# One value group for all tokens in the first stage of a one-core decoder layer, the other group per half of the tokens

## The chip, the cores and the metric

The program runs on one core of one Trainium2 chip. The metric is the device time of one execution in microseconds (us): the kernel before takes 1529.22 us, the median of three runs (1527.17 to 1531.24). Of five engines, PE (TensorE) multiplies matrices into PSUM banks, DVE (VectorE) and POOL (GpSimd) do elementwise work, ACT (ScalarE) evaluates functions and copies, and SP (SyncE) issues nearly all DMAs. Each engine takes its instructions in a fixed order; so does SP's queue.

## What is computed

One layer over 1024 tokens of width 2048, conditioned by a vector c, all in float32:

```python
mod = silu(c) @ w_ada + b_ada
shift, scale, gate = split(mod, 3)
h = rms_norm(x, norm_g) * (1 + scale) + shift
u_a, v_a, z_a, q, k, v, z_b = split(h @ w_in)
y_a = u_a * (W_s LN(v_a) + b_s)
y_b = sliding_window_attention(rope(q), rope(k), v, sinks)
y = concat(y_a * silu(z_a), y_b * silu(z_b))
x = x + gate * (y @ w_out)
out = rms_norm(x, final_norm_g) * (1 + scale_f) + shift_f
```

LN is a layer norm over the 1024 columns of v_a (the "value columns" here); W_s mixes positions inside chunks of 128 tokens.

## The kernel before

**Arithmetic.** A float32 product is made of three faster ones: each operand is split into a rounded high part (ACT, a copy) and a low part (the difference, DVE or POOL), and `mm3` (lines 205 to 208) issues high x high, high x low and low x high into one bank. A projection of one 512-column group for one half (512 tokens) takes 16 steps of 128 input features (kt), each step 4 banks x 3 = 12 matmuls of 512 columns. `split_w` (lines 138 to 150) makes the parts of a weight step in three rotating buffers `wh`/`wl`; `chunk` (line 127) loads the weights of two steps by one 512 KB DMA.

**Stages.** The input tiles Hh, Hl (high and low) of only one half fit, so the halves run one after the other. At the start the modulation is not yet known: `scale` and `shift` are sums over 16 x 1 MB of w_ada that DVE makes step by step (`mod_col`, line 155, two multiply-and-sum instructions on line 165 per step, the data in ring buffers of 512 KB).

- The first stage (lines 655 to 675) projects half 0 for both value groups va0 and va1 as soon as each `scale` column is there: per kt the scale sums, the x tile, its split (lines 664 and 665), and two weight steps. The low weight parts of va0 go to POOL (from kt 2), those of va1 to DVE. It uses x * g * scale without the norm and the shift. Both are put in later: `norm_v` (line 438) multiplies by the row norm rx and adds the row shift @ W (the "correction"), on line 447, for half 0 only. Eight DMAs of rows of x also run here, for the norm (`x_stat`, line 170).
- Then `spread` (line 187) turns the norms into a tile, and the second stage (lines 690 to 695) projects kv and q0 with the full h, while `shift` is summed.
- `half(h)` (line 747) does q1, for half 1 also va0 and va1, then zb0, zb1, u0, u1, za0, za1 and the output projection.

**Order of the work.** Attention is a generator of 32 units (plus 3 steps to drain) that runs between the projection steps: `tick` (line 242) adds a credit per step, from kt 6 of q1 on, and lets one unit go when it reaches 1; the credit is 0.74 in half 0 and 0.58 in half 1 (line 774). A unit is scores (335, 336), soft-max (339 to 348), transposes (355), a split (359, 360) and values (367 to 376). A second queue of background work, `bg` (line 257), takes one step per two kt, by the lists `bgn`: first `corr_bg` (line 711: 16 loads of va weights, 32 sums on line 723, four loads of quarters of the shift row, then the sums become a row through bank `pv_bank`, which the attention's values also use), then `gate_bg` (32 sums, then a row through the bank mm[3]), then the x rows of half 1. A scheduler then sets each engine's order from the program order and priorities.

In half 0 all low weight parts from q1 to u0 are made on POOL (`lo_pool`), otherwise on DVE.

Of the kernel before, what the change touches and what calls it, by code (L numbers as in the profile page):

```python
# [10 lines left out]
F32 = mybir.dt.float32  # L11
# [4 lines left out]
P = 128  # L16
# [15 lines left out]
def R(t):  # L32
    return t.bitcast(F32R)
# [3 lines left out]
def hybrid_layer(ctx: ExitStack, tc: tile.TileContext, A, out):  # L37
# [7 lines left out]
    def st(shape, name):  # L45
        return sb.tile(shape, F32, tag=name, name=name)
# [391 lines left out]
    def norm_v(h):  # L438
        assert not waiting
        if h == 0:  # L440
            for i in range(2):
                load_row(4, i, zz[i])
        for t in range(4):
            va = [Y[t][:, i, :] for i in range(2)]
            if h == 0:
                for i in range(2):
                    dve.scalar_tensor_tensor(va[i], va[i], rx[0][:, t:t + 1], zz[i], op0=ALU.mult, op1=ALU.add)
                yield
# [81 lines left out]
    x_d = dram.tile([4, P, D], F32, name="x_d")  # L530
    r0 = st([P, 4], "rs0")
# [117 lines left out]
    acc, rb, sq = F[8], F[9], F[10:12]  # L649
    rings.extend(Y[1:4])  # L650
    raws.append(Y[0])

    stat0 = (None for t in range(4) for _ in x_stat(0, t))

    def g1_kt(kt):
# [9 lines left out]
        dve.scalar_tensor_tensor(R(Hl[kt]), X[kt], a, Hh[kt], op0=ALU.mult, op1=ALU.subtract)  # L665
        if kt >= 7:
            next(stat0, None)
        if kt == KT - 1:
            for _ in stat0:
# [3 lines left out]
    vb = project(["va0", "va1"], ["mm", "att"], per_kt=g1_kt, pool_lo=("va0",),  # L673
                 steps=[(kt, g) for kt in range(KT - 2) for g in ("va0", "va1")]
                 + [(kt, g) for g in ("va0", "va1") for kt in (KT - 2, KT - 1)])
    raws, rings = deque(w_raw), deque(ring)

    def g1_evac(i, t):
        grab(Y[t][:, i, :], vb[("va0", "va1")[i]][t])

    g1_evac(0, 0)
    with tc.high_priority():
        b = banks8["mm"][0]
        spread(rx[0], b, rb, sq[0])
    for i in range(2):
        for t in range(4):
            if i + t:
                g1_evac(i, t)
# [13 lines left out]
    def gate_bg():  # L702
        for kt in range(KT):
            yield from mod_col("gate", kt, gate_c[:, kt:kt + 1])
        to_row(0, gate_c, banks8["mm"][3])
# [5 lines left out]
    def corr_bg():  # L711
        to_row(3, shift_c, sc_bank[0])
        for pc in range(4):
            load_row(3, pc, misc)
            for c2 in range(4):
# [31 lines left out]
    def half(h, kq):  # L747
# [24 lines left out]
        def start(kt):  # L772
            if kt == 6:
                credit[0], credit[1] = 0.0, (0.74 if h == 0 else 0.58)
# [3 lines left out]
        if h:  # L778
            for i, g in enumerate(("va0", "va1")):
                ps = project([g], ["mm"], bgn=(0, 1))[g]  # L780
                for t in range(4):
                    grab(Y[t][:, i, :], ps[t])
# [130 lines left out]
```

## Time and profile before

| what | value |
|---|---|
| median of three runs | 1529.22 us |
| the profiled execution | 1529.09 us, span 1527.3 us |
| PE busy | 1457.6 us (95%), 7049 matmuls |
| DVE, ACT, POOL busy | 985.6, 630.9, 227.7 us |
| DMA | 284.85 MB, mean 187 GB/s |
| chain that ended last | PE 48%, issue 30%, DVE 10%, DMA 6% |

Matmuls are pipelined, so a busy PE in the table is not a PE at full rate: what counts is the time between the starts of two matmuls, and the idle stretches. "Granted clock" is the share of full TensorE speed; it has two levels, 1.0 (2.4 GHz) and 0.5 (1.2 GHz).

### The profile page before, as it was taken

What the parts mean: (1) busy time and instruction counts of PE and PEld (TensorE: products, weight loads), DVE (VectorE), ACT (ScalarE), POOL (GpSimd) and SP (SyncE); (2) the same over time, 40 slices, a digit from 0 to 9 for tenths busy, and PEclk for the clock granted to TensorE, in tenths of its full rate; (3) what the DMA queues carried; (4) which work ended last, traced back from release to release, by engine and by line L of the source; (5) the groups of instructions that cost most, each with busy time, mean ns of one, the idle gap of its engine ahead of it and who ended that gap; (6) DMA issues with size and microseconds to landing.
All of it is one profiled execution on the core that took longest, in us unless ns stands there. A gap on an engine that the chain in (4) does not pass through costs nothing.

```text
span 1527.3 us, 20341 instructions
## 1 busy us (share of the span) xinstructions
PE 1457.6 (95%) x7049; PEld 1209.2 (79%) x7049; DVE 985.6 (65%) x1953; ACT 630.9 (41%) x1397; POOL 227.7 (15%) x168
## 2 busy tenths in 40 slices
PE   7989999898899999999999999999999999999997
PEld 5768778676788887778889788788878888888897
DVE  6779864989854555533566578888755554456456
ACT  3443245566552233243343246566632222332341
POOL 1212154335341010000001010000011000010002
PEclk9999999999999999999999999999999999999999
DMA  9987855555334657665467664444355665565422
GB/s 364 354 286 240 266 185 154 169 179 183 86 120 147 198 181 237 212 206 171 158 191 232 193 208 143 124 138 124 120 186 181 204 203 190 173 226 194 136 86 111
DMA packets 89258, 284.85 MB, mean 187 GB/s; under 512 B 12145, under 2 KB 12737, under 8 KB 89154
## 3 DMA queue, kind: packets, MB, share of 16 engines
q1 hardware_dynamic: 89010, 283.02, 57.2%
q8 instruction: 55, 0.90, 0.2%
q10 hardware_dynamic: 144, 0.52, 0.1%
q14 instruction: 49, 0.40, 0.1%
HBM read 257.24 MB, written 13.67 MB: 177 GB/s over the span
## 4 chain that ended last, share of the span: by engine, by line
PE 48%; issue 30%; DVE 10%; DMA 6%; POOL 3%; ACT 2%; SPq 0%; DVEq 0%; POOLq 0%; ACTq 0%
PE mm L206 13%; PE mm L208 13%; PE mm L207 13%; DMA ring<-ada 2%; PE att L208 2%; PE att L207 2%; PE att L206 2%; DVE ring L165 1%; DVE ring L723 1%; PE att L355 1%; POOL wl L149 1%; DMA wr<-win 1%; DVE wl L149 1%; DVE t L339 1%; PE att L466 1%
## 5 line engine op out<-in xcount | busy, mean ns | idle before, releaser
L208 PE MATMUL mm<-r,wl 128*128 128x512 f32 x1024 | 402.6, 393 | 6.9 <-DVE wl L149 3.5
L206 PE MATMUL mm<-r,wh 128*128 128x512 f32 x1024 | 404.5, 395 | 1.1 <-ACT wh L148 0.4
L207 PE MATMUL mm<-r,wh 128*128 128x512 f32 x1024 | 402.8, 393 | 0.0
L148 ACT ACTIVATE wh<-wr 128x512 fp32r<-128x512 f32 x318 | 197.5, 627 | 332.2 <-PE mm L207 189.4
L149 DVE TENSOR_TENSOR wl<-wr,wh 128x512 fp32r<-128x512 f32 x226 | 164.6, 732 | 138.1 <-ACT wh L148 133.3
L208 PEld LDWEIGHTS mm<-r,wl 128*128 128x128 f32 x1024 | 194.2, 190 | 51.6 <-DVE wl L149 5.9
L206 PEld LDWEIGHTS mm<-r,wh 128*128 128x128 f32 x1024 | 194.2, 190 | 41.4 <-ACT y L285 1.3
L207 PEld LDWEIGHTS mm<-r,wh 128*128 128x128 f32 x1024 | 194.4, 190 | 37.5
L206 PE MATMUL mm<-wh,r 128*128 128x512 f32 (+1 forms) x448 | 170.5, 383 | 14.8 <-ACT r L664 12.0
L207 PE MATMUL mm<-wl,r 128*128 128x512 f32 (+1 forms) x448 | 171.2, 382 | 2.8 <-POOL wl L149 2.5
L148 ACT ACTIVATE wh<-ring 128x512 fp32r<-128x512 f32 x138 | 86.7, 629 | 207.4 <-PE mm L207 129.0
L149 POOL TENSOR_TENSOR wl<-wr,wh 128x512 fp32r<-128x512 f32 x92 | 129.5, 1411 | 283.1 <-ACT wh L148 237.7
L208 PE MATMUL mm<-wh,r 128*128 128x512 f32 (+1 forms) x448 | 168.4, 380 | 0.0
L207 PE MATMUL att<-wl,r 128*128 128x512 f32 (+1 forms) x448 | 161.3, 360 | 1.9 <-DVE wl L149 1.9
L208 PE MATMUL att<-wh,r 128*128 128x512 f32 (+1 forms) x448 | 160.8, 359 | 0.0
L206 PE MATMUL att<-wh,r 128*128 128x512 f32 (+1 forms) x448 | 160.7, 359 | 0.0
L149 DVE TENSOR_TENSOR wl<-ring,wh 128x512 fp32r<-128x512 f32 x138 | 97.7, 711 | 94.8 <-ACT wh L148 86.9
L206 PEld LDWEIGHTS mm<-wh,r 128*128 128x128 f32 x448 | 85.7, 192 | 35.1 <-ACT r L664 15.6
L480 POOL TENSOR_TENSOR y<-y,t 128x512 f32<-128x512 f32 x32 | 47.7, 1514 | 396.3 <-ACT t L489 351.1
L207 PEld LDWEIGHTS mm<-wl,r 128*128 128x128 f32 x448 | 85.9, 192 | 19.8 <-POOL wl L149 4.5
L208 PEld LDWEIGHTS mm<-wh,r 128*128 128x128 f32 x448 | 85.9, 192 | 16.0 <-DVE r L665 0.6
L207 PEld LDWEIGHTS att<-wl,r 128*128 128x128 f32 x448 | 84.4, 188 | 17.5 <-DVE wl L149 3.9
(207 smaller groups left out, 1984.2 us busy)
## 6 DMA issues: line engine op xcount, KB each, us to landing
wr<-win SPq DMA_DIRECT2D x124, 512.0 KB, 4.3
ring<-ada SPq DMA_DIRECT2D x90, 512.0 KB, 5.1
wr<-ada SPq DMA_DIRECT2D x55, 512.0 KB, 4.3
ring<-win SPq DMA_DIRECT2D x46, 512.0 KB, 3.8
wr<-wout SPq DMA_DIRECT2D x38, 512.0 KB, 3.7
ring<-wout SPq DMA_DIRECT2D x26, 512.0 KB, 3.7
y<-xn SPq DMA_DIRECT2D x20, 512.0 KB, 5.1
ring<-wvaT SPq DMA_DIRECT2D x16, 512.0 KB, 5.4
```

The costliest lines, as they stand in the source:

```text
L148: act.activation(R(w_hi[i]), r[:, kk, :], AF.Copy)
L149: (pool if on_pool else dve).tensor_tensor(R(w_lo[i]), r[:, kk, :], w_hi[i], op=ALU.subtract)
L165: dve.tensor_tensor_reduce(w, w, cb[:, c0:c0 + n], scale=1.0, scalar=prev, op0=ALU.mult, op1=ALU.add, accum_out=o)
L206: pe.matmul(o, lhsT=lh, rhs=rh, start=first, stop=False)
L207: pe.matmul(o, lhsT=lh, rhs=rl, start=False, stop=False)
L208: pe.matmul(o, lhsT=ll, rhs=rh, start=False, stop=last)
L339: dve.tensor_tensor_reduce(ps[i], os[i], mk, scale=-0.125, scalar=nsnk[:, h0 + i:h0 + i + 1], op0=ALU.add, op1=ALU.min, accum_out=nm[:, i: ...
L355: pe.transpose(pt_bank[:, c:c + P], p[:, 256 * i + P * j:256 * i + P * j + P], ident)
L466: pe.matmul(b[:, t * P:t * P + P], lhsT=Y[t][:, g // 4, (g % 4) * P:(g % 4) * P + P], rhs=wsp[:, g * P:g * P + P], start=True, stop=True)
L480: pool.tensor_tensor(y, y, zz[c], op=ALU.mult)
L723: dve.tensor_tensor_reduce(ti, ti, misc, scale=1.0, scalar=prev, op0=ALU.mult, op1=ALU.add, accum_out=acc_)
```

## The change

The first stage now projects va0 alone, but for both halves: x of both halves is loaded, scaled and split at each kt (`other` holds the parts of half 1), and one weight step serves both. Half 1's result is written to DRAM (`v_d`) and read back in half 1. The group va1 is projected in each half between q1 and zb0, with the full h, so it needs no correction. va0 is corrected in both halves, so the correction covers 512 columns (8 loads, 16 sums) and not 1024. The credit is 0.58 in both halves. The gate row goes through the bank `pv_bank` and, since the background list is shorter by 8 and half 0 longer by 8 calls, it falls into za0. All low parts of the first stage's weights from kt 2 on are POOL's.

```diff
--- before.py
+++ after.py
@@ -437,15 +437,11 @@
 
     def norm_v(h):
         assert not waiting
-        if h == 0:
-            for i in range(2):
-                load_row(4, i, zz[i])
+        load_row(4, 0, zz[0])
         for t in range(4):
             va = [Y[t][:, i, :] for i in range(2)]
-            if h == 0:
-                for i in range(2):
-                    dve.scalar_tensor_tensor(va[i], va[i], rx[0][:, t:t + 1], zz[i], op0=ALU.mult, op1=ALU.add)
-                yield
+            dve.scalar_tensor_tensor(va[0], va[0], rx[h][:, t:t + 1], zz[0], op0=ALU.mult, op1=ALU.add)
+            yield
             stt, mv, rs = sm(12, "bst"), sm(2, "mv"), sm(1, "rs")
             for i in range(2):
                 dve.bn_stats(stt[:, 6 * i:6 * i + 6], va[i])
@@ -528,6 +524,7 @@
         mm3(ps, R(Hh[f])[:, tk], R(Hl[f])[:, tk], Wh, Wl, first, last)
 
     x_d = dram.tile([4, P, D], F32, name="x_d")
+    v_d = dram.tile([4, P, 512], F32, name="v_d")
     r0 = st([P, 4], "rs0")
 
     def rows_bg(Am, Bm):
@@ -646,10 +643,11 @@
     dve.tensor_scalar(cols[:, C_B + 48:C_B + 64], cols[:, C_B + 48:C_B + 64], 1.0, None, op0=ALU.add)
 
     X = [F[i // 2] if i % 2 == 0 else Y[4 + i // 4][:, (i // 2) % 2, :] for i in range(KT)]
-    acc, rb, sq = F[8], F[9], F[10:12]
+    rb, sq, x1 = F[9], F[8:9], [F[8], F[10], F[11]]
     rings.extend(Y[1:4])
     raws.append(Y[0])
 
+    vb, other = [four("mm"), four("att")], {}
     stat0 = (None for t in range(4) for _ in x_stat(0, t))
 
     def g1_kt(kt):
@@ -663,6 +661,11 @@
         dve.tensor_tensor(a, a, cols[:, C_G + kt:C_G + kt + 1], op=ALU.mult)
         act.activation(R(Hh[kt]), X[kt], AF.Copy, scale=a)
         dve.scalar_tensor_tensor(R(Hl[kt]), X[kt], a, Hh[kt], op0=ALU.mult, op1=ALU.subtract)
+        x, hi, lo = x1[kt % 3], alr(), alr()
+        sp.dma_start(out=x, in_=A["xT"][1, kt])
+        act.activation(R(hi), x, AF.Copy, scale=a)
+        dve.scalar_tensor_tensor(R(lo), x, a, hi, op0=ALU.mult, op1=ALU.subtract)
+        other[kt] = hi, lo
         if kt >= 7:
             next(stat0, None)
         if kt == KT - 1:
@@ -670,22 +673,38 @@
                 pass
             stats(0)
 
-    vb = project(["va0", "va1"], ["mm", "att"], per_kt=g1_kt, pool_lo=("va0",),
-                 steps=[(kt, g) for kt in range(KT - 2) for g in ("va0", "va1")]
-                 + [(kt, g) for g in ("va0", "va1") for kt in (KT - 2, KT - 1)])
+    def va_mm(h, kt, W):
+        hi, lo = other[kt] if h else (Hh[kt], Hl[kt])
+        for t in range(4):
+            tk = slice(t * P, t * P + P)
+            mm3(vb[h][t], R(hi)[:, tk], R(lo)[:, tk], W[0], W[1], kt == 0, kt == KT - 1)
+        if h:
+            frr(*other.pop(kt))
+
+    last = []
+    for kt in range(KT):
+        g1_kt(kt)
+        if kt % 2 == 0:
+            raw = chunk(A["win"][GI["va0"], kt // 2])
+        W = split_w(raw, kt % 2, on_pool=kt > 1)
+        if kt < KT - 2:
+            for h in range(2):
+                va_mm(h, kt, W)
+        else:
+            last.append((kt, W))
+    for h in range(2):
+        for kt, W in last:
+            va_mm(h, kt, W)
     raws, rings = deque(w_raw), deque(ring)
 
-    def g1_evac(i, t):
-        grab(Y[t][:, i, :], vb[("va0", "va1")[i]][t])
-
-    g1_evac(0, 0)
     with tc.high_priority():
-        b = banks8["mm"][0]
-        spread(rx[0], b, rb, sq[0])
-    for i in range(2):
-        for t in range(4):
-            if i + t:
-                g1_evac(i, t)
+        grab(Y[0][:, 0, :], vb[0][0])
+        spread(rx[0], vb[0][0], rb, sq[0])
+    for t in range(1, 4):
+        grab(Y[t][:, 0, :], vb[0][t])
+    for t in range(4):
+        grab(Y[t][:, 1, :], vb[1][t])
+        sp.dma_start(out=v_d[t], in_=Y[t][:, 1, :])
 
     def g2_kt(kt):
         for _ in mod_col("shift", kt, shift_c[:, kt:kt + 1]):
@@ -702,7 +721,7 @@
     def gate_bg():
         for kt in range(KT):
             yield from mod_col("gate", kt, gate_c[:, kt:kt + 1])
-        to_row(0, gate_c, banks8["mm"][3])
+        to_row(0, gate_c)
 
     def stat_bg():
         for t in range(4):
@@ -712,7 +731,7 @@
         to_row(3, shift_c, sc_bank[0])
         for pc in range(4):
             load_row(3, pc, misc)
-            for c2 in range(4):
+            for c2 in range(2):
                 t = next_ring()
                 sp.dma_start(out=t, in_=A["wvaT"][pc, c2])
                 for i in range(2):
@@ -771,15 +790,15 @@
 
         def start(kt):
             if kt == 6:
-                credit[0], credit[1] = 0.0, (0.74 if h == 0 else 0.58)
+                credit[0], credit[1] = 0.0, 0.58
 
         q1 = project(["q1"], ["mm"], bgn=(0, 1) if h else (1,), after_kt=start)["q1"]
         q_grab(q1, (2, 3))
-        if h:
-            for i, g in enumerate(("va0", "va1")):
-                ps = project([g], ["mm"], bgn=(0, 1))[g]
-                for t in range(4):
-                    grab(Y[t][:, i, :], ps[t])
+        ps = project(["va1"], ["mm"], bgn=(0, 1) if h else (1,))["va1"]
+        for t in range(4):
+            grab(Y[t][:, 1, :], ps[t])
+            if h:
+                sp.dma_start(out=Y[t][:, 0, :], in_=v_d[t])
         silu_gate(project(["zb0"], ["mm"], bgn=(0, 1) if h else (1, 1, 1, 1, 1, 1, 2, 1))["zb0"], 4, 16)
         ln = norm_v(h)
 
```

**VectorE, first stage, kt 5 to 7** (ISA is the multiply-and-sum of line 165). Before:

```order
L165 ISA ring_95,scale_c<-ring_95,cb,pc_s_276 128x1024
L165 ISA scale_c 128x1
L663 TENSOR_TENSOR scale_c<-scale_c,cols 128x1
L665 SCALAR_TENSOR_TENSOR r_151<-t_127,scale_c,r_150 128x512
L149 TENSOR_TENSOR wl_101<-y_116,wh_98 128x512
L165 ISA ring_96,pc_s_195<-ring_96,cb,cols 128x1024
L165 ISA pc_s_195 128x1
L165 ISA y_117,scale_c<-y_117,cb,pc_s_195 128x1024
L165 ISA scale_c 128x1
L149 TENSOR_TENSOR wl_100<-y_116,wh_97 128x512
L663 TENSOR_TENSOR scale_c<-scale_c,cols 128x1
L665 SCALAR_TENSOR_TENSOR r_153<-y_121,scale_c,r_152 128x512
```

Now:

```order
L663 SCALAR_TENSOR_TENSOR r_159<-y_121,scale_c,r_158 128x512
L667 SCALAR_TENSOR_TENSOR r_161<-t_135,scale_c,r_160 128x512
L165 ISA ring_94,pc_s_277<-ring_94,cb,cols 128x1024
L165 ISA pc_s_277 128x1
L165 ISA ring_95,scale_c<-ring_95,cb,pc_s_277 128x1024
L165 ISA scale_c 128x1
L661 TENSOR_TENSOR scale_c<-scale_c,cols 128x1
L663 SCALAR_TENSOR_TENSOR r_163<-t_127,scale_c,r_162 128x512
L667 SCALAR_TENSOR_TENSOR r_165<-t_132,scale_c,r_164 128x512
L165 ISA ring_96,pc_s_196<-ring_96,cb,cols 128x1024
L165 ISA pc_s_196 128x1
L165 ISA y_117,scale_c<-y_117,cb,pc_s_196 128x1024
```

The two splits of va1's weights (`wl`), which stood between the sums, are gone; each kt now is two sums, one small product and two splits of x (lines 663 and 667).

**TensorE, where the correction's sums become a row** (L195), in half 0. Before:

```order
L335 MATMUL att_68<-k_2_105,r_172 128x256
L336 MATMUL att_68<-k_2_109,r_172 128x256
L335 MATMUL att_68<-k_2_105,r_173 128x256
L355 MATMUL att_69<-ident,t_128 128x128 x3
L195 MATMUL att_70<-ident,corr 16x128
L355 MATMUL att_69<-ident,t_128 128x128
L336 MATMUL att_68<-k_2_109,r_173 128x256
L206 MATMUL mm_63<-r_142,wh_99 128x512
L367 MATMUL att_70<-r_170,v_112 128x256
L368 MATMUL att_70<-r_171,v_112 128x256
```

Now:

```order
L206 MATMUL mm_63<-wh_99,r_140 128x512
L207 MATMUL mm_63<-wl_102,r_140 128x512
L208 MATMUL mm_63<-wh_99,r_141 128x512
L195 MATMUL att_70<-ident,corr 16x128
L206 MATMUL mm_64<-wh_99,r_140 128x512
L207 MATMUL mm_64<-wl_102,r_140 128x512
L367 MATMUL att_70<-r_152,v_114 128x256
L368 MATMUL att_70<-r_153,v_114 128x256
L367 MATMUL att_70<-r_152,v_115 128x256
```

Before, 1272 projection matmuls and 61 transposes (L355) stand ahead of this row in PE's order; now 1179 and 20. Of units' transposes none stand between row 1152 and row 1257 of PE's order now, and those of the next five units within about 100 rows behind.

**TensorE, where the gate sums become a row.** Before, in the output projection of half 0:

```order
L207 MATMUL att_70<-wl_102,r_160 128x512
L208 MATMUL att_70<-wh_99,r_161 128x512
L195 MATMUL mm_66<-ident,gate_c 16x128
L206 MATMUL mm_63<-wh_97,r_172 128x512
L207 MATMUL mm_63<-wl_100,r_172 128x512
```

Now, in za0:

```order
L207 MATMUL mm_66<-r_145,wh_97 128x512
L208 MATMUL mm_66<-r_144,wl_100 128x512
L195 MATMUL att_70<-ident,gate_c 16x128
L206 MATMUL mm_63<-r_138,wh_98 128x512
L207 MATMUL mm_63<-r_139,wh_98 128x512
```

The row went through mm_66, a bank that the matmuls just behind it fill; now through att_70, while those behind it fill mm_63 to mm_66.

## Rows read from the trace of the kernel before

**Rows 1.** Windows over all engines (start:end us; length; busy us by engine; clock; DMA)

```profile
58.37:117.33 58.96, 50.52 (x200) 38.34 (x201) 42.52 (x67) 26.21 (x45) 12.04 (x9) 0.94 0.82 299
252.00:438.00 186.00, 165.31 (x856) 135.50 (x855) 160.44 (x457) 119.40 (x346) 78.23 (x58) 0.97 0.50 149
913.00:1118.00 205.00, 199.43 (x1043) 168.75 (x1042) 167.89 (x472) 132.18 (x363) 15.70 (x12) 0.99 0.44 133
654.00:668.00 14.00, 11.51 (x45) 8.86 (x44) 2.36 (x4) 4.12 (x8) 0.00 (x0) 0.88 0.64 206
```

**Rows 2.** Timeline of TensorE, 11 to 118 us (start us, us, operation)

```profile
12.35 0.80 PE L206 MATMUL mm<-wh,r 128*128 128x512 f32 x1 [6.33 <-ACT r L664]
...
105.37 0.80 PE L206 MATMUL mm<-wh,r 128*128 128x512 f32 x1 [2.86 <-ACT r L664]
...
110.65 1.39 PE L191 MATMUL mm<-t,ones 128*128 128x128 f32 x8
...
112.11 0.40 PE L207 MATMUL att<-wl,r 128*128 128x512 f32 x1
...
117.33 0.39 PE L206 MATMUL att<-r,wh 128*128 128x512 f32 x1
```

**Rows 3.** Timeline of VectorE in the first stage, 64 to 92 us

```profile
66.38 1.28 DVE L165 CUSTOM_DVE_ANT_0 y<-y,cb,cols 128x1024 f32<-128x1024 f32 x1
...
69.98 0.75 DVE L665 SCALAR_TENSOR_TENSOR r<-t,scale_c,r 128x512 fp32r<-128x512 f32 x1 [0.79 <-ACT r L664]
72.74 0.69 DVE L149 TENSOR_TENSOR wl<-y,wh 128x512 fp32r<-128x512 f32 x1 [2.01 <-ACT wh L148]
73.35 2.32 DVE L165 CUSTOM_DVE_ANT_0 ring<-ring,cb,cols 128x1024 f32<-128x1024 f32 x1
...
76.03 0.69 DVE L149 TENSOR_TENSOR wl<-y,wh 128x512 fp32r<-128x512 f32 x1 [0.35 <-ACT wh L148]
```

**Rows 4.** Timeline of ScalarE in the same stretch

```profile
75.37 0.63 ACT L148 ACTIVATE wh<-y 128x512 fp32r<-128x512 f32 x1 [2.65 <-PE mm L208]
78.16 0.72 ACT L664 ACTIVATE r<-y,scale_c 128x512 fp32r<-128x512 f32 x1 [2.16 <-DVE scale_c L663]
...
91.36 0.72 ACT L664 ACTIVATE r<-y,scale_c 128x512 fp32r<-128x512 f32 x1 [2.16 <-DVE scale_c L663]
```

**Rows 5.** Timeline of VectorE, 97 to 103 us

```profile
98.93 2.91 DVE L189 TENSOR_SCALAR t<-ident,rx 128x128 f32<-128x128 f32 x4 [1.14 <-POOL rx L185]
```

**Rows 6.** Waits of TensorE, 117 to 216 us (us in total, times, longest us)

```profile
PE att L208 <- DVE wl L149: 2.8, 6, 1.3
```

**Rows 7.** Waits of TensorE, 252 to 438 us

```profile
PE att L355 <- ACT t L347: 6.0, 2, 3.1
PE att L355 <- DVE r L360: 5.4, 6, 2.3
PE att L355 <- DVE t L348: 3.8, 1, 3.8
```

**Rows 8.** Groups of VectorE, 252 to 438 us (busy us, mean ns; idle before)

```profile
L723 DVE CUSTOM_DVE_ANT_0 ring<-ring,t,corr 128x512 f32<-128x512 f32 x24 | 23.8, 1006 | 4.1 <-DMA t<-rows_d 2.3 <-DMA ring<-wvaT 1.8
```

**Rows 9.** Line 723: the correction's sums (first and last start us)

```profile
L723 DVE DVE_READ_ACCUMULATOR2_ANT corr<- x32: 73/77/85, 282.9 to 355.4; 128x1 f32 x32
L723 DVE CUSTOM_DVE_ANT_0 ring<-ring,t,corr x24: 725/744/1855, 297.8 to 354.7; 128x512 f32<-128x512 f32 x24
```

**Rows 10.** Timeline of SyncE's queue, 240 to 356 us

```profile
274.43 0.34 SPq L202 DMA_DIRECT2D t<-rows_d  x1
...
292.49 0.33 SPq L202 DMA_DIRECT2D t<-rows_d  x1
```

**Rows 11.** Waits of TensorE, 580 to 670 us

```profile
PE mm L206 <- ACT row_s L197: 2.5, 1, 2.5
PE att L207 <- DVE wl L149: 1.9, 3, 1.3
```

**Rows 12.** Timeline of ScalarE, 655 to 664 us

```profile
658.72 1.06 ACT L174 ACTIVATE wr<-wr 128x1024 f32<-128x1024 f32 x1 [5.16 <-DMA wr<-xn]
```

## The prediction

> **What bounds the kernel now.** I read the page first: PE is busy for most of the span, so its full rate and its idle time are the two questions. The windows [rows 1] show, stage by stage, PE's busy time against the stretch, the granted clock and what DVE does. Full rate comes from PE's timeline [rows 2]: between 112.11 and 117.33 us lie 23 starts, so a matmul of 512 columns takes 0.227 us, and a kt of the first stage (24 of them) 5.45 us. The change removes no matmul and adds none, so it can only win idle time, clock and queueing. These I look for in three places.
>
> First stage: 12.35 to 117.33 us is 105.0 us [rows 2] for 384 matmuls, 87.2 us at full rate. The loss sits late. ACT's x splits come at 78.16 and 91.36 [rows 4], so two kt take 13.20 us where PE needs 10.9. DVE's timeline [rows 3] shows why: its order holds a weight split of va1 that waits 2.01 us for ACT, and a second one (76.03) that waits for an ACT split which itself waits 2.65 us for PE to free a buffer [rows 4]. The next scale sums stand behind it, so PE waits for DVE, which waits for PE.
>
> Attention of half 0, 252 to 438 us: PE is idle for 186.0 - 165.3 = 20.7 us with a clock of 0.97, against 205.0 - 199.4 = 5.6 us and 0.99 in half 1's attention [rows 1]. The waits end at the soft-max and the split on ACT and DVE [rows 7], and DVE is busy 160.4 of 186 us (86%), against 167.9 of 205 (82%) in half 1.
>
> Output projection of half 0: one wait of 2.5 us, for the copy of the gate row [rows 11], because ACT had stood 5.16 us before a load of x rows [rows 12].
>
> **The change part by part**, against the profiled execution's 1529.1 us (0.1 below the median of the runs, so the sums serve for both).
>
> *First stage.* Per kt ACT keeps three copies and DVE five operations: a split of x replaces a weight split of va1; the bytes stay equal (256 KB of x for 256 KB of weights). What goes is the loop through PE. Gain if PE then runs at full rate: 2.3 us in each of three pairs, 1.9 in the kt that opens the pattern (my estimate, half a pair's loss rounded up for its first wait), and the half clock of kt 15, whose 12 matmuls take 5.28 us, from 105.37 to the spread at 110.65 [rows 2], where 2.7 would do: 6.9 + 1.9 + 2.6 = 11.4 us. The first matmul comes later, because the second x tile is split ahead of the weights on ACT: one x split and one copy, 0.72 + 0.63 us [rows 4], leaves 10.0. Now DVE: from one first sum to the x split 3.6 us, then two splits of 0.75: 5.1 us per kt [rows 3], just under PE's 5.45. But a sum took 2.32 us instead of 1.28 beside POOL's split, once per pair: 0.5 us per kt, 5.6 in all, 0.15 us over PE for some nine kt, 1.4 us. Last, the four small products for the spread now share a buffer with half 1's x, so they follow the split of kt 15; before, they and a wait for POOL took 2.91 and 1.14 us ahead of kt 15's sums [rows 5]. PE may wait 0 to 3 us for them; I take 1. Sum: **-7.5 us**, bounds -10 and -1 (DVE 0.65 us over PE per kt, spread late).
>
> *Second stage.* The four stores of half 1's result stand in SP's queue before the shift loads of kt 2 and wait for ACT's last copies. This stage already waits 2.8 us for splits behind such sums [rows 6]. Bounds 0 and +4; I take **+1.5**, near the row.
>
> *Attention of half 0.* 16 of 32 sums go: 16 x 1.0 us of DVE [rows 8]; four corrections of 0.75 us go. 16 POOL splits come, each of which may hold up a DVE operation by up to 1.04 us (2.32 less 1.28) [rows 3]; I take half, 8 us. DVE's work falls from 160 to about 149 us. The attention's transposes now spread over 636 projection matmuls in PE's order (1008 to 1644), before over 492 (996 to 1488): 144 x 0.227 = 33 us more cover. So DVE is at 149 of 208 us, 72%, under half 1's 82%. At half 1's idle and clock the gain is 15.1 + 3.5 = 18.6 us. Against it: no unit stands ahead of the correction row, and the next five units stand close, by the matmuls between them about 2.5 us apart, which is less than a unit's chain through ACT and DVE; 3 us. And the row itself: PE reaches it 93 matmuls and some ten units (1.5 us each, an estimate) earlier, 37 us, that is at 355.4 - 3.8 - 37 = 314 us on the old clock [rows 7, 9]. The sums need four quarter rows one after the other; one let the sums go on at 297.8, 5.3 us after its issue at 292.49 [rows 9, 10], and four sums take 4: 9.3 us. From the first sum at 282.9 that is 4 + 3 x 9.3 = 32 us, 315 us. They meet; a wait of 4.5 us, about as now (3.8) [rows 7], stays. **-11 us**, bounds -18.6 and 0.
>
> *Gate row.* No matmul behind it uses its bank, and its sums move out of the output projection: the waits of 2.5 and 1.9 us [rows 11] and the clock of 0.88 over 14 us [rows 1], 1.7 us, go: 6.1. The same sums now stand in u1 to za1, where they may cost some: **-5**, bounds -6.1 and 0.
>
> *Half 1.* It loses 16 weight splits with their matmuls to the first stage, so its density stays. New are four corrections (3 us of DVE) and a row load in zb1, while attention runs, and eight cheap DMAs read and write the stored half. **+2**, bounds 0 and +8.
>
> Sum: -7.5 + 1.5 - 11 - 5 + 2 = -20: **1509 us**.
>
> **The rivals.** *POOL's splits block DVE* (0.15). The sum of 2.32 us [rows 3] may be met by every split once DVE has no idle time: 6.1 us per kt, the first stage gains 3 less 0 to 1, and half 0 pays 16.6 us of DVE and not 8. Some 7 us of the forecast are lost: 1516. Against it: DVE has 1.04 us of slack elsewhere in a pair. By the Trainium skill, page "SBUF — State Buffer", section "SBUF: two separate sides", the two engines share one port pair under an exclusive lock, and a VectorE operation with two SBUF inputs and a GpSimd operation wait for each other's end. By that rule this rival is the rule, not the exception; the trace agrees with it in the one sum per pair.
>
> *All goes well* (0.13): -10 + 0 - 18.6 - 6.1 + 0 = -34.7, 1494.
>
> *The attention isn't spread alike after all* (0.13): the credit is a wish, the scheduler's order has a hole before the correction row and a bunch behind it. Then half 0 keeps its idle time: 1520.
>
> *The correction comes late and the kernel is slower* (0.07). Two quarter rows came 18.1 us apart [rows 10]. If that is the pace of the row loads in SP's queue, and not of the four weight loads per quarter that halve, the sums end at 282.9 + 4 + 3 x 18.1 = 341 us and PE stands 27 us at the row, ACT behind it, and a stretch of half clock follows (1.7 us): 1509 + 27 - 3 + 1.7 = 1535. It decides above some 15 us per quarter. Against it: four loads into three buffers per quarter explain 18 us.
>
> **How the numbers follow.** The forecast has 0.47, its own range 1502 to 1516; 0.05 is left for what I don't see. The range 1495 to 1521 leaves out half of the good rival, the slow one and the edges. 0.3%, 4.6 us, is about what a measurement of this kernel can tell from no change: faster takes the forecast, the first three rivals but for an edge of the third: 0.87. The same 0.06, slower 0.07.
>
> **What would show it.** The second stage's first matmul near 110 us instead of 117.33; DVE's order in 64 to 92 us without a wait for `wh`; PE's idle time in half 0's attention near 10 us in a stretch of some 208; a transposed correction with no wait over 5 us ahead of it; no wait for `row_s` in the output projection. The forecast is wrong if PE still waits for x splits every second kt, or if a single wait of over 10 us stands before the correction row.

## The result, and the profile after

The changed kernel takes 1517.55 us, the median of six runs (1515.64 to 1519.9), beside 1528.2 us before; the ratio is 0.9931, 95% interval 0.9915 to 0.9948. That is 11 us, about half of the 20 that were forecast, and inside the range. The profiled execution has a span of 1515.1 us (1527.3 before).

Where it lies is read from the starts of the 6144 projection matmuls in TensorE's timelines, cut at the same count in both kernels, so that each stretch holds the same number of matmuls (attention and spatial mixing of half 0 lie wholly in the fourth). The names are those of the changed kernel; before, the fourth stretch ends with u1 and the fifth with the last output group of half 0:

| stretch (matmuls) | before | after | difference | forecast |
|---|---|---|---|---|
| span start to the first matmul | 12.4 | 13.9 | +1.5 | +1.4 |
| first stage (1 to 385) | 105.0 | 98.9 | -6.1 | -8.9 |
| second stage (385 to 865) | 97.0 | 96.8 | -0.2 | +1.5 |
| q1 to the end of u0 (865 to 1825) | 306.2 | 308.3 | +2.2 | -11 |
| to the last but one output group (1825 to 2977) | 271.4 | 261.3 | -10.1 | -5 |
| last output group and half 1 (2977 to 6144) | 725.3 | 725.8 | +0.5 | +2 |

So the total hides two errors of opposite sign: half 0's attention won nothing, and the stretch behind it won twice what was forecast. Of these 10.1 us the cut itself makes about one: the last output group takes 44.6 us in both kernels, where 192 matmuls at full rate take 43.5, and it lies in the fifth stretch before the change and behind it after.

Windows over all engines, after (columns as in [rows 1]): the first stage from 58.37 us on, the attention of half 0, and the fifth stretch of the table.

```profile
58.37:112.78 54.41, 49.88 (x212) 39.69 (x211) 42.59 (x66) 27.19 (x48) 16.07 (x9) 0.97 0.86 322
250.00:471.00 221.00, 198.87 (x1001) 164.98 (x1000) 163.44 (x453) 127.03 (x360) 92.17 (x68) 0.96 0.52 158
517.92:779.19 261.27, 261.27 (x1154) 216.27 (x1153) 108.06 (x166) 86.92 (x155) 12.47 (x9) 1.00 0.53 167
```

In the last row PE is busy for all of the 261.27 us at full clock: what could be won there has been. In the attention VectorE is at 163 of 221 us, 74%, as forecast (149 of 208, 72%; before 86%), but PE is still idle for 22.1 us (20.7 before) with a lower clock, 0.96. The forecast had the share right and the idle time wrong. The share was luck: VectorE's work is 14 us more than forecast, in a stretch 13 us longer.

TensorE's timeline, after, answers to [rows 2]: first matmul, two starts a pair of kt apart, the late one in kt 14, the second stage's first.

```profile
13.89 0.79 PE L206 MATMUL mm<-wh,r 128*128 128x512 f32 x1 [7.58 <-ACT wh L148]
...
73.35 0.84 PE L206 MATMUL mm<-wh,r 128*128 128x512 f32 x3
...
85.08 0.86 PE L206 MATMUL mm<-wh,r 128*128 128x512 f32 x3
...
100.09 0.80 PE L207 MATMUL mm<-wl,r 128*128 128x512 f32 x1 [2.42 <-POOL wl L149]
...
112.78 0.39 PE L206 MATMUL att<-r,wh 128*128 128x512 f32 x1
```

Two kt take 11.73 us now (13.20 before, 10.9 at full rate). VectorE's timeline over that pair, after (answers to [rows 3]):

```profile
72.26 1.28 DVE L165 CUSTOM_DVE_ANT_0 ring<-ring,cb,cols 128x1024 f32<-128x1024 f32 x1
...
73.58 2.18 DVE L165 CUSTOM_DVE_ANT_0 y<-y,cb,pc_s 128x1024 f32<-128x1024 f32 x1
...
75.81 1.12 DVE L661 TENSOR_TENSOR scale_c<-scale_c,cols 128x1 f32<-128x1 f32 x1
77.72 0.75 DVE L663 SCALAR_TENSOR_TENSOR r<-y,scale_c,r 128x512 fp32r<-128x512 f32 x1 [0.79 <-ACT r L662]
...
81.70 0.16 DVE L661 TENSOR_TENSOR scale_c<-scale_c,cols 128x1 f32<-128x1 f32 x1
```

No wait for `wh` is left. But VectorE has no other gap than 0.79 us per kt before the first split, and two operations of a pair are drawn out, a sum (2.18 us, others 1.28) and the small product (1.12, else 0.16). So VectorE looks like the bound; the run pipe tests it. TensorE waits 0.55 us once in this pair, for POOL's low weight part and not for an x split.

Waits of TensorE in the attention of half 0, after (answers to [rows 7]):

```profile
PE att L355 <- DVE r L360: 14.0, 6, 4.5
PE att L195 <- DVE corr L742: 4.3, 1, 4.3
```

The wait before the correction row is as forecast (4.5). The long soft-max waits of before are gone, and waits for the low split of the transposed probabilities (line 360) have taken their place. Three are long, 4.47 us ending at 282.39, 4.05 at 366.06 and 4.27 at 416.83. VectorE's timeline shows what stood ahead of that split each time:

```profile
279.46 0.69 DVE L742 CUSTOM_DVE_ANT_0 ring<-ring,t 128x512 f32<-128x512 f32 x1 [3.48 <-DMA t<-rows_d]
...
281.91 0.42 DVE L360 TENSOR_TENSOR r<-att,r 128x256 fp32r<-128x256 f32 x1
...
361.05 2.15 DVE L165 CUSTOM_DVE_ANT_0 ring<-ring,cb,pc_s 128x1024 f32<-128x1024 f32 x1 [1.00 <-DMA ring<-ada]
...
363.13 2.27 DVE L165 CUSTOM_DVE_ANT_0 ring<-ring,cb,cols 128x1024 f32<-128x1024 f32 x1
...
365.33 0.68 DVE L360 TENSOR_TENSOR r<-att,r 128x512 fp32r<-128x512 f32 x1
...
407.75 3.46 DVE L443 SCALAR_TENSOR_TENSOR y<-y,rx,t 128x512 f32<-128x512 f32 x2 [1.44 <-DMA t<-rows_d]
...
413.62 2.44 DVE L453 TENSOR_SCALAR y<-y,mv_s,rs_s 128x512 f32<-128x512 f32 x3 [0.44 <-POOL rs_s L450]
416.09 0.69 DVE L360 TENSOR_TENSOR r<-att,r 128x512 fp32r<-128x512 f32 x1
```

First the correction's sums after a load of the shift row, then two gate sums, then steps of the norm. The gate sums should not be there by the forecast. POOL's timeline beside them, and TensorE's:

```profile
360.82 3.50 POOL L149 TENSOR_TENSOR wl<-wr,wh 128x512 fp32r<-128x512 f32 x2 [3.23 <-ACT wh L148]
```

```profile
366.06 0.69 PE L355 MATMUL att<-ident,t 128*128 128x128 f32 x2 [4.05 <-DVE r L360]
```

Beside POOL's two splits the two sums take 2.15 and 2.27 us instead of 1.28, so some 1.9 us of that wait may be POOL's (an estimate from these rows).

Groups of VectorE in the attention, after, from 250 to 453 us (answers to [rows 8]):

```profile
L165 DVE CUSTOM_DVE_ANT_0 ring<-ring,cb,cols 128x1024 f32<-128x1024 f32 x10 | 13.8, 1377 | 0.5 <-DMA ring<-ada 0.5
L165 DVE CUSTOM_DVE_ANT_0 ring<-ring,cb,pc_s 128x1024 f32<-128x1024 f32 x8 | 12.7, 1586 | 2.3 <-DMA ring<-ada 2.3
L742 DVE CUSTOM_DVE_ANT_0 ring<-ring,t,corr 128x512 f32<-128x512 f32 x12 | 9.5, 832 | 9.0 <-DMA t<-rows_d 9.0
L742 DVE CUSTOM_DVE_ANT_0 ring<-ring,t 128x512 f32<-128x512 f32 x4 | 2.5, 689 | 3.5 <-DMA t<-rows_d 3.5
```

Sixteen sums of the correction went, and sixteen of the gate came (18 stand here, 2 before): the background list has 8 calls in q1, 8 in va1 and 9 in zb0, and the correction now needs only 8 loads of them. The sums cost 38.5 us of VectorE here; before it was 31.3 for the correction, 24 of whose 32 sums stand in [rows 8], and two gate sums.

### The profile page after: what moved, and what is told of

The parts are those of the page before. It is cut to its first block, busy times and chain, and to the rows that moved or that the text cites. A ratio compares the mean times of both kernels' runs of the same rounds, so it can differ in the third digit from the quotient of the medians.

```text
span 1515.1 us, 20294 instructions
## 1 busy us (share of the span) xinstructions
PE 1447.4 (96%) x7049; PEld 1208.2 (80%) x7049; DVE 960.8 (63%) x1905; ACT 629.8 (42%) x1397; POOL 256.2 (17%) x184
## 5 line engine op out<-in xcount | busy, mean ns | idle before, releaser
L148 ACT ACTIVATE wh<-wr 128x512 fp32r<-128x512 f32 x324 | 201.7, 627 | 355.7 <-PE mm L207 195.2
L208 PEld LDWEIGHTS mm<-r,wl 128*128 128x128 f32 x1024 | 192.9, 188 | 55.1 <-DVE wl L149 8.7
L149 DVE TENSOR_TENSOR wl<-wr,wh 128x512 fp32r<-128x512 f32 x220 | 154.8, 708 | 127.6 <-ACT wh L148 117.2
L149 POOL TENSOR_TENSOR wl<-wr,wh 128x512 fp32r<-128x512 f32 x104 | 151.3, 1459 | 293.8 <-ACT wh L148 271.6
L149 DVE TENSOR_TENSOR wl<-ring,wh 128x512 fp32r<-128x512 f32 x120 | 88.5, 741 | 89.7 <-ACT wh L148 86.4
L148 ACT ACTIVATE wh<-ring 128x512 fp32r<-128x512 f32 x120 | 75.0, 627 | 150.0 <-PE mm L207 66.6
L207 PEld LDWEIGHTS mm<-wl,r 128*128 128x128 f32 x448 | 86.1, 192 | 22.3 <-POOL wl L149 7.5
L206 PEld LDWEIGHTS att<-wh,r 128*128 128x128 f32 x448 | 84.5, 189 | 13.9
```

What stands on the lines that cost most here:

```text
L148: act.activation(R(w_hi[i]), r[:, kk, :], AF.Copy)
L149: (pool if on_pool else dve).tensor_tensor(R(w_lo[i]), r[:, kk, :], w_hi[i], op=ALU.subtract)
L206: pe.matmul(o, lhsT=lh, rhs=rh, start=first, stop=False)
L207: pe.matmul(o, lhsT=lh, rhs=rl, start=False, stop=False)
L208: pe.matmul(o, lhsT=ll, rhs=rh, start=False, stop=last)
```

## The experiments

Theory A: in the attention single blocks in VectorE's queue set PE's idle time, among them the gate sums that moved up; in the first stage VectorE is the bound. The rivals are that POOL's splits hold VectorE up everywhere, that the density of the units decides, and, for the gate row, that its place decides and not its bank. The ratio is to the kernel before; stretches come from one profile each, cut as above. The rows come from different chips, on which the kernel before has medians of 1525.85 to 1529.21 us, so the ratios are to be compared and not the medians.

| kernel | median us | ratio, 95% interval | first stage | 865 to 1825 | 1825 to 2977 |
|---|---|---|---|---|---|
| changed | 1517.55 | 0.9931, 0.9915 to 0.9948 | 98.9 | 308.3 | 261.3 |
| gate_late | 1508.93 | 0.9901, 0.9867 to 0.9936 | 97.5 | 300.3 | 265.4 |
| nocorr | 1507.03 | 0.9871, 0.9842 to 0.9899 | 99.1 | 295.0 | 261.3 |
| va1d | 1515.6 | 0.9933, 0.9911 to 0.9956 | 99.1 | 307.0 | 261.3 |
| c74 | 1517.73 | 0.9948, 0.9926 to 0.9969 | 97.5 | 311.1 | 261.3 |
| pipe | 1511.01 | 0.9898, 0.987 to 0.9926 | 91.8 | 310.5 | 261.3 |
| tail | 1514.97 | 0.9921, 0.9894 to 0.9947 | 94.8 | 309.8 | 261.3 |
| b_bank | 1527.44 | 0.9994, 0.9976 to 1.0011 | 104.7 | 309.2 | 268.5 |
| rows_zz | 1516.03 | 0.9918, 0.9888 to 0.9948 | 99.1 | 307.5 | 261.3 |
| gate_u0 | 1527.51 | 0.9987, 0.997 to 1.0004 | 99.1 | 307.0 | 269.0 |
| norm | 1519.68 | 0.9932, 0.9909 to 0.9955 | 99.1 | 308.5 | 261.3 |
| all_five | 1521.58 | 0.9951, 0.9934 to 0.9968 | 91.0 | 306.1 | 269.5 |
| best | 1503.46 | 0.9836, 0.9821 to 0.9851 | 90.8 | 294.6 | 266.9 |

Kernels that are alike up to a point differ there by chance: 97.5 to 99.1 us for the first stage of those that leave it alone, and 94.5 to 96.8 for the second stage, which no experiment edits (nocorr has 100.5, but gate sums moved into it, see there). The stretch 865 to 1825 takes 306.2 and 309.2 us in the kernel before and b_bank, 308.3 to 310.5 in changed, pipe and tail, and 300.3 and 294.6 in gate_late and best, and within each of these groups its code is the same. So 3 us there prove nothing, and the size of a larger difference is known only to some us. (The 301 us of some expectations run from the 961st to the 1921st matmul; there gate_late took 293.2, gate_u0 299.7, all_five 298.1 and best 287.1.)

**gate_late.** The gate row now falls into the output projection and passes through a bank that is being filled, so part of a column group is lost.

```diff
-  ps = project(["va1"], ..., bgn=(0, 1) if h else (1,))
+  ps = project(["va1"], ..., bgn=(0, 1) if h else (1, 0, 0, 0, 0, 0, 0, 0))
-  project(["zb0"], ..., bgn=(0, 1) if h else (1, 1, 1, 1, 1, 1, 2, 1))
+  project(["zb0"], ..., bgn=(0, 1) if h else (0,))
```

> The changed kernel, with no background steps in va1 and zb0 of half 0 but the one that makes the correction row, so that the gate sums start after the attention, in u1, as they did before the change. Theory A (the shorter correction let 18 gate sums, 26.5 us of VectorE, move up into the attention of half 0, where they replace the 16 correction sums that went): VectorE's work between 243.6 and 457 us falls from 156 to about 130 us, the wait of 4.2 us at 366 us goes with its stretch of half clock, PE idle time in that stretch falls from 22 to 15 us or less; but the gate sums come back to the stages from u1 on and cost there some 3 to 4 us of waits for low weight parts, as before the change. In all 1511 to 1517 us. Theory B (POOL's 16 more splits hold up VectorE, whatever it does): idle time stays within 2 us of 22, and the run is at 1518 to 1522 us, since only the later waits are added.

Window of the attention and TensorE's waits in it:

```profile
245.00:459.00 214.00, 199.59 (x1006) 166.19 (x1005) 140.94 (x422) 127.05 (x360) 88.29 (x70) 0.95 0.42 124
```

```profile
PE att L355 <- DVE r L360: 8.6, 3, 4.1
PE att L195 <- DVE corr L742: 5.2, 1, 5.2
```

VectorE's work falls by 22 us and PE's idle time from 22.1 to 14.4; the stretch wins 8.0 us. All of it lies in one group: the 192 matmuls of zb0, where 13 of the gate sums stood, take 55.1 us for 64.4. Behind the stretch 4.2 us come back. Theory A holds for the gate sums. The median lies below theory A's range. By the ratios the whole wins 4.6 us, about what the two stretches give, but the intervals overlap.

**nocorr.**

```diff
-  load_row(3, pc, misc)
...
-  t = next_ring()
-  sp.dma_start(out=t, in_=A["wvaT"][pc, c2])
-  for i in range(2):
+  for i in range(0):
```

> The changed kernel without the correction's loads and sums: 8 weight loads, 16 sums and four loads of quarters of the shift row are left out, so the correction is a row of zeros; the background steps stay, so the gate sums stand where they stood. Theory A (waits come from single places where the correction's sums or its row stand ahead of a unit): the waits of 4.6 us at 282 us and 4.4 us at 308 us go, with some 10 us of half clock behind them (5 us lost): 1505 to 1510 us. Theory B (POOL's splits): the sums held up POOL's and VectorE's other work by little, 1514 to 1518 us.

Waits of TensorE in the attention:

```profile
PE att L355 <- DVE r L360: 10.4, 3, 4.3
PE att L195 <- DVE y L376: 1.8, 1, 1.8
```

The time is theory A's, and the stretch wins 13.3 us. But the edit moved the gate sums too, which were expected to stay: without the correction's work ahead of them 18 start between 204 and 346 us (308 to 396 in the changed kernel), four in the second stage, two in q1, 11 in va1 and one in zb0. Of the 13.3 us zb0 gives 9.3 (55.1 us, as in gate_late), and va1, where the correction's sums stood, 5.5; q1 takes 2.0 back. The second stage loses 3.7: TensorE waits 2.3 us at 206.7 for a weight split behind the first of these sums. So only about 5 us are the correction's. Its sums had kept VectorE busy for 12.0 us and standing before loads for 12.5 (the two groups of line 742), with whatever stood behind them; a share of busy time of 74% doesn't show that. Three waits behind other blocks remain, the norm's among them.

**va1d** and **c74**, the two rivals.

```diff
+  lo_pool[0] = False
   ps = project(["va1"], ...)
...
+  lo_pool[0] = h == 0
   silu_gate(project(["zb0"], ...)
```

> The changed kernel with the 16 low weight parts of va1 in half 0 made on VectorE instead of POOL. Theory A: VectorE pays 16 x 0.7 us and is freed of being held; the waits at the four places (282, 308, 366, 417 us) stay: within 3 us of 1517.5. Theory B (each POOL split holds VectorE by up to 1.04 us, which the prediction took by half): VectorE is freed of up to 16 us, PE idle time in the attention of half 0 falls by 5 us or more, 1508 to 1513 us.

```diff
-  credit[0], credit[1] = 0.0, 0.58
+  credit[0], credit[1] = 0.0, (0.74 if h == 0 else 0.58)
```

> The changed kernel with the old credit of 0.74 in half 0, so that the 32 units again end after 492 and not 636 projection matmuls. The prediction held that 33 us more cover are worth something like 8 to 10 us. Theory A (the waits stand at single places, not where units are dense): within 3 us of 1517.5. If the spread is worth what was forecast, 1525 to 1528 us.

Both stay within 3 us of the changed kernel, where theory A put them. Windows of the attention, va1d and then c74:

```profile
246.00:467.00 221.00, 201.69 (x1008) 166.72 (x1008) 169.12 (x470) 127.72 (x361) 70.35 (x54) 0.95 0.51 159
```

```profile
243.00:433.00 190.00, 167.72 (x844) 137.93 (x843) 159.62 (x433) 118.37 (x344) 76.60 (x53) 0.95 0.54 164
```

Without 22 us of POOL's work PE is idle for 19.3 us, and three of the four long waits stay (the first, at 282 us, does not). This clears POOL's splits of va1 only: no run took those of zb0 away, which draw out the gate sums there. With VectorE at 84% it is idle for 22.3 us, just as at 74%: spreading the units, the term that was to bring most, is worth the 2.7 us of the stretch at best, which is within the scatter.

**pipe.** With `red[0]` the last sum issued:

```diff
   act.activation(R(hi), x, AF.Copy, scale=a)
+  if 5 <= kt < KT - 1:
+      next(sums[kt + 1])
+  with tc.issue_after(red[0].ins) if kt >= 5 else nullcontext():
       (the two splits of x)
```

> The changed kernel with another order on VectorE in the first stage: from kt 5 on, the first scale sum of the next kt stands between the small product and the two x splits, so that ScalarE's copy runs under it (the 0.79 us for which VectorE stands before the first split of each kt). Theory A (VectorE sets the pace of kt 6 to 14: 11.73 us for two kt, of which 1.58 are that standing and 1.87 two operations held up by POOL's weight split): two kt take 10.9 us, TensorE's own time, and the second stage begins 3 to 4 us sooner. Theory B (the pace comes from DMA or from POOL's splits, which reach TensorE 0.7 to 0.8 us late every second kt): two kt stay at 11.5 us or more, less than 1 us won. In all 1513 to 1515 us by A, 1517 to 1518 by B.

VectorE's timeline over a pair (line 667 was 661, 673 was 663):

```profile
72.19 0.74 DVE L673 SCALAR_TENSOR_TENSOR r<-y,scale_c,r 128x512 fp32r<-128x512 f32 x1
...
73.52 1.27 DVE L167 CUSTOM_DVE_ANT_0 ring<-ring,cb,pc_s 128x1024 f32<-128x1024 f32 x1
...
75.57 1.28 DVE L167 CUSTOM_DVE_ANT_0 ring<-ring,cb,cols 128x1024 f32<-128x1024 f32 x1 [0.58 <-DMA ring<-ada]
...
79.53 1.77 DVE L167 CUSTOM_DVE_ANT_0 y<-y,cb,pc_s 128x1024 f32<-128x1024 f32 x1 [1.34 <-DMA y<-ada]
...
81.35 1.12 DVE L665 TENSOR_TENSOR scale_c<-scale_c,cols 128x1 f32<-128x1 f32 x1
```

The standing before the splits is gone, and VectorE now waits for DMA instead: it has time over. Kt 6 to 13 take 43.5 us, which is 192 matmuls at full rate, against 47.8. So theory A holds, VectorE was the bound. The first stage wins 7.0 us, more than it asked, since the end of the stage is 2.9 us shorter too.

**tail.**

```diff
-  W = split_w(raw, kt % 2, on_pool=kt > 1)
+  W = split_w(raw, kt % 2, on_pool=1 < kt < KT - 2)
```

> The changed kernel with the low weight parts of the last two kt of the first stage on VectorE instead of POOL, where they stand behind the power of the row norms (1.99 us). Theory A (that power makes TensorE wait 2.6 us at 97.3 us, and the half clock of 3.4 us that follows costs 1.7): the wait and the half clock go, VectorE pays 1.4 us: 2 to 4 us faster, 1513.5 to 1515.5 us. Theory B (the splits would be late anyway, since VectorE ends kt 15 late): within 1 us, 1516.5 to 1518.5 us.

POOL's timeline, the changed kernel and then this one:

```profile
96.48 1.99 POOL L185 TENSOR_TENSOR rx<-v_s,mhalf 128x4 f32<-128x4 f32 x1 [7.84 <-DVE v_s L184]
98.45 2.83 POOL L149 TENSOR_TENSOR wl<-y,wh 128x512 fp32r<-128x512 f32 x2
```

```profile
96.35 1.03 POOL L185 TENSOR_TENSOR rx<-v_s,mhalf 128x4 f32<-128x4 f32 x1 [7.84 <-DVE v_s L184]
```

From the first matmul of kt 14 to the second stage it is 11.8 us for 15.9, and the wait of 2.42 us with its half clock is gone (kernels that leave the end of the stage alone take 14.5 to 16.2). Theory A; in the time of the whole the intervals overlap.

**b_bank**, one line of the change in the kernel before.

```diff
-  to_row(0, gate_c, banks8["mm"][3])
+  to_row(0, gate_c)
```

> The kernel before with one line of the change: the gate row goes through the bank of the attention's values and no longer through a bank that the matmuls behind it fill. Its place in the output projection stays; that bank holds a column group there, so the row spoils a part of it. Theory A (the bank made the wait of 2.5 us and the half clock behind it): 4.3 us of the output projection go, 1524 us. Theory B (the place, not the bank: the waits for low weight parts in u1 to za1 and for ScalarE come from the late sums and the loads beside them): within 1.5 us of before, 1527 to 1529 us.

Waits of TensorE from 520 to 795 us:

```profile
PE att L207 <- DVE wl L149: 2.9, 3, 1.5
PE mm L208 <- DVE wl L149: 0.8, 1, 0.8
```

The wait for the row is gone and 2.9 us of the stretch with it, of theory A's 4.3; the splits' waits stay. In the time of the whole this can't be seen: the median lies where theory B put it. So of the 10.1 us that the stretch won, some 3 are the bank's, by one profile.

**rows_zz** and **norm**, two attempts at the other blocks.

```diff
-  load_row(3, pc, misc)
+  q = load_row(3, pc, zz[pc])
...
-  dve.tensor_tensor_reduce(ti, ti, misc, ...
+  dve.tensor_tensor_reduce(ti, ti, q, ...
```

> The changed kernel with the four quarters of the shift row loaded into four buffers (zz) and not one after the other into one, so the correction's sums no longer wait for the sums ahead of them and a load. Theory A (the row loads' 9 to 10 us per quarter hold VectorE's queue 12.4 us and put the wait of 4.3 us before the correction row): that wait goes, the sums end 10 us or more sooner, 4 to 6 us faster: 1511.5 to 1513.5 us. Theory B (the five units bunched behind the row cost as much as the wait itself): they move to the row's new place and 2 us or less are won, 1515.5 to 1518 us.

```diff
   to_row(4, corr)
+  load_row(4, 0, misc)
...
-  load_row(4, 0, zz[0])
```

> The changed kernel with the corrected row for the norm of the value columns loaded right after it is made, into another buffer, and not when the norm begins. Theory A (the load, 1.44 us late, piles the norm's steps up on VectorE, 3.46 and 1.27 and 2.44 us together, and that block makes the wait of 4.4 us at 417 us): the wait shrinks to 2 us or less, its half clock goes, 1513 to 1515.5 us. Theory B (the norm's steps stand close in VectorE's order whatever the load does): the wait stays at 3.5 us or more, within 1.5 us of 1517.5.

Waits of TensorE in the attention of rows_zz:

```profile
PE att L355 <- DVE r L360: 10.8, 5, 4.0
PE att L367 <- DVE y L376: 3.4, 5, 1.5
...
PE att L195 <- DVE corr L742: 1.8, 1, 1.8
```

The wait for the row shrinks to 1.8 us, and five short ones of the bunched units come: theory B. In norm (where half 1 does not load its row) the wait of 4.27 us becomes one of 3.2 us, from 386.5 us on, where the norm now stands among two gate sums; that is between the two theories' bounds, and without a gain, as in theory B.

**gate_u0** and **all_five**, the misses.

```diff
   (as gate_late)
-  ps = project(["u0"], ["mm"], bgn=(h,))["u0"]
+  ps = project(["u0"], ["mm"], bgn=(1,))["u0"]
```

> The changed kernel with the gate sums started in u0 (one stands in va1), so that their row falls into za1, ahead of the output projection, and spoils nothing. Theory A: as in gate_late the attention keeps 6 to 8 us (the stretch from the end of q1's matmuls to the end of u0's, 301 us in the changed kernel, is 293 to 296 us), and since the sums now end before the output projection, the 4 us that came back there in gate_late stay away: 1508 to 1512 us. Theory B (what gate_late won came from its spoiled row or by chance): the stretch stays at 299 us or more, 1515 us or more.

By the ratio it came out 8.6 us above the changed kernel, with 299.7 us for the stretch: the numbers of theory B. But the edit did not do what it was made for. The scheduler set the eight sums that the program has in u0 ahead, into zb0. Two of VectorE's lines there:

```profile
339.32 2.02 DVE L165 CUSTOM_DVE_ANT_0 ring<-ring,cb,cols 128x1024 f32<-128x1024 f32 x1 [0.27 <-DMA ring<-ada]
...
392.17 1.29 DVE L165 CUSTOM_DVE_ANT_0 ring<-ring,cb,cols 128x1024 f32<-128x1024 f32 x1 [0.54 <-DMA ring<-ada]
```

The matmuls of zb0 run from 334.5 to 398.1 us, 63.6 us, and u0 takes the 52.3 us of the changed kernel. So the run puts back into zb0 what gate_late took away, the gain goes with it, and the run speaks for theory A of gate_late. All kernels with the change agree: zb0 takes 63.1 to 70.2 us where 8 or 13 gate sums stand in it, and 55.1 us each time where one or none does (nocorr, gate_late, best).

The sums do end sooner than in gate_late, but the row falls to the last step of za1, and TensorE has it among the first matmuls of the output projection, which fill its bank. TensorE's timeline there, and ScalarE's:

```profile
645.81 0.27 PE L195 MATMUL att<-ident,gate_c 128*16 128x128 f32 x1
...
652.94 0.50 PE L206 MATMUL att<-wh,r 128*128 128x512 f32 x1 [4.78 <-ACT row_s L197]
```

```profile
649.15 1.06 ACT L174 ACTIVATE wr<-wr 128x1024 f32<-128x1024 f32 x1 [5.50 <-DMA wr<-xn]
...
652.64 0.25 ACT L197 ACTIVATE row_s<-att 16x128 f32<-16x128 f32 x1
```

This is [rows 11, 12] again, in another bank: ScalarE stands before a load of x rows, the row's copy stands behind it, and TensorE waits for the bank, 4.8 us. The profiled execution (span 1521.9 us) is 6.8 us longer than that of the changed kernel; the stretch behind the attention has 7.7 of them (269.0 for 261.3). Neither theory had this wait.

> The changed kernel with the five edits together: the first stage's other order on VectorE, its last two low parts on VectorE, the gate sums from u0 on, the four quarter rows in four buffers and the early load for the norm. If the single gains stand at different places and add up: first stage 90 to 92 us (98.8 in the changed kernel), the stretch from q1 to u0 288 to 292 us (301), 1497 to 1502 us. If the attention's waits only move to the next late operation: that stretch 294 to 297 us, 1503 to 1507 us.

The first stage won what it should (91.0), but the edit of gate_u0 again put eight sums into zb0 (63.3 us) and brought the same wait for the row: the attention stretch won only 2 us, and the one behind it lost 8.2. The last stretch took 735.8 us, 10 more than in the changed kernel; in norm, whose edit it shares, it took 731.8, and 723.4 to 729.0 elsewhere. That loss is unassigned. Neither expectation held.

**best.** pipe, tail and gate_late, with the row in the bank of before and VectorE as its copier:

```diff
-  to_row(0, gate_c)
+  to_row(0, gate_c, banks8["mm"][3], True)
...
+  if on_dve:
+      dve.tensor_scalar(t, bank[:KT, :P], 1.0, None, op0=ALU.mult)
```

> The changed kernel with the edits of pipe, tail and gate_late together, and the gate row through the fourth bank of the group that stands free there (as before the change), copied out by VectorE, which does not stand before a load of x rows as ScalarE does. If the three gains lie at different places: first stage 91 us (98.8 in the changed kernel), the stretch from the end of q1's matmuls to u0 293 us (301), output projection as in gate_late (stretch of 178 us), 1500 to 1504 us. If the copy of the row makes TensorE wait as before the change (4.3 us with its half clock): 1504.5 to 1508 us. If the attention gives back what the first stage wins, since DMA and VectorE run ahead of one another differently: 1509 us or more.

Windows, attention and first stage, and TensorE's waits from 495 to 762 us:

```profile
241.00:448.00 207.00, 195.48 (x1002) 162.81 (x1001) 140.46 (x421) 126.69 (x360) 88.77 (x68) 0.98 0.43 128
13.45:104.26 90.81, 90.81 (x393) 74.83 (x393) 80.81 (x126) 42.37 (x72) 22.36 (x13) 1.00 0.98 375
```

```profile
PE att L212 <- DVE wl L149: 2.7, 3, 1.3
PE mm L213 <- DVE wl L149: 0.7, 1, 0.7
```

The first stage has no idle time at full clock, PE is idle for 11.5 us in the attention, and no wait for the row is left. 0.9836 (0.9821 to 0.9851) beats both kernels: 25 us below the one before.

## Why the prediction was right and wrong

- **First stage** (forecast -7.5, measured -4.6 with the later start). The loop through PE was the loss, and it is gone; the first matmul came 1.5 us later, as reckoned. TensorE does not wait for x splits every second kt, the sign that was named for being wrong. Two terms were mis-sized. In a pair I let one sum be held, by 1.04 us; both POOL splits of a pair hold something, 0.90 and 0.96 us, and VectorE needs 11.7 us for two kt. That term, put at 1.4 us, came to 4.3 (kt 6 to 13 take 47.8 us for 43.5 in pipe). So the rival "POOL's splits block DVE" happened here, with 5.9 us per kt for its 6.1. By the rule of the Trainium skill (page "SBUF — State Buffer", section "SBUF: two separate sides") that was to be expected, and the trace agrees, with 2.18 us for 1.28. And at the end I priced the small products of the spread at 1 us; they took 0.87 us and made nobody wait, while POOL's power of the row norms, which I had not moved in the list, stood before the last weight splits: 2.42 us and a half clock (tail).
- **Second stage** (+1.5, measured -0.2). Unedited runs of it scatter by 2.3 us (94.5 to 96.8), so nothing is shown either way, nor of the stores in SP's queue.
- **Attention of half 0** (-11, measured +2.2). The step "16 of 32 sums go" failed: with 8 background calls more and 8 steps less, 16 gate sums more took their place (18 for 2). I had read this change only at the row's end of the list. Worth 8 us (gate_late), with the scatter of some us. The other half of the term, 33 us more cover at half 1's idle time, failed too: density doesn't set the idle time (c74), and even with 16 of the gate sums gone PE is idle for 14.4 us (gate_late) where half 1 has 5.6. POOL's splits of va1, priced at 8 us of VectorE's work, moved the stretch by 1.3 us (va1d), which the scatter covers; those of zb0 were not tested. The correction row's part, "a wait of 4.5 us stays", was right: 4.3, and the sums took from 279.5 to 308.5 us, 29 for a forecast of 32, so the slower rival, 18 us per quarter row, fell. The rival "the attention isn't spread alike" gave nearly the time that came (1520), for another reason: denser units cost 2.7 us at most (c74), the blocks in VectorE's queue much.
- **Gate row** (-5, measured -10.1 in its stretch, about 1 of it by the cut). The mechanism of the bank was right, about 3 us (b_bank). Another 4.2 us came since 18 of the 32 sums no longer stood behind the attention (gate_late puts 16 back): the sentence that they "now stand in u1 to za1" was wrong by these. Some 2 us stay unassigned; the upper bound of 6.1 summed only the waits of one window.
- **Half 1** (+2, measured +0.5, or about -0.5 without the cut's 1). Not shown either way: kernels with no edit in half 1 take 723.4 to 729.0 us for this stretch, so +2 can't be told from nothing.

Both large errors have one root for the most part, the place of the gate sums, and they partly cancelled: what the stretch behind the attention won by it, the attention paid, and more. That the total came out at half of the forecast is luck to that extent. Of the signs that were named, no wait for `wh` in VectorE's first stage, no wait over 5 us ahead of the correction row and none for `row_s` came true; the second stage begins at 112.78 us, not near 110, and PE's idle time in the attention is 22.1 us, not near 10.

## What to carry to other kernels

When a change shortens a list of background work, read what moves up into the freed places, and price that beside what goes. In an in-order queue a block of background work can cost its length where a short operation of the critical chain stands behind it, whatever the engine's busy share says; so move blocks, and don't only spread the chain. Then look in the trace where the moved work really stands: a scheduler can put it ahead of its place in the program (gate_u0). A row that goes through a bank should have a copier that doesn't stand before a load.

## What the runs showed beside

A POOL operation drew out even a product of 128x1 on VectorE, 1.12 us for 0.16. And one and the same stretch of code took 300.3 us in one kernel and 294.6 in another (gate_late and best, 865 to 1825), so a gain of a few us in one stage needs more than one profile.
